# Fetching split keys and queries as float32 on both sides, rows outermost, on GpSimd's queue

## Chip, cores and metric

The kernel runs on one core of a Trainium2 chip. The metric is the device time of one execution in microseconds (us), the median of several runs; lower is better. TensorE (PE) does matrix products, VectorE (DVE) and ScalarE (ACT) the arithmetic on tiles, GpSimd (POOL) some of it too. SP, ACT and POOL each have a queue that issues DMA transfers, and 16 DMA engines carry them out.

## Reference

Two transformer blocks, batch 1, 1024 tokens, width 1024, float32. The first has two kinds of attention side by side (a latent one over all keys, "MLA", and a dilated window one), then a mixture of 16 experts. The second block is run twice ("layers"); each layer has three kinds of attention over 1024 tokens and 256 context tokens: a differential one, one with grouped queries, one with a neighbourhood window on a grid. Cut to the three that matter here:

```python
def diff_attend(q, k, v, lam):
    s = jnp.einsum('bqhmd,bkhmd->bhmqk', q, k).astype(jnp.float32) * (q.shape[-1] ** -0.5)
    p = jax.nn.softmax(s, axis=-1)
    a = (p[:, :, 0] - lam * p[:, :, 1]).astype(v.dtype)
    return jnp.einsum('bhqk,bkhd->bqhd', a, v)

def gqa_attend(q, k, v):
    ...
    s = jnp.einsum('bqhgd,bkhd->bhgqk', qg, k).astype(jnp.float32) * (d ** -0.5)
    p = jax.nn.softmax(s, axis=-1).astype(v.dtype)
    o = jnp.einsum('bhgqk,bkhd->bqhgd', p, v)
```

The softmax is sharp on these inputs, so scores are computed to nearly full float32: every query and key is split into a high part and a low part (float32r, the form that TensorE takes at full rate), and a score is a sum of products of the parts.

## The kernel before

**Split and stack.** The projections write the parts to DRAM. `stack_out` (L654) transposes a tile of queries or keys, rounds it to float32r (`H`), takes the rest (`L`), and SP stores both in DRAM arrays `st[key]`, declared float32, shaped [2 parts, blocks, 128 rows, tokens]. The keys are "Dq", "Dk" (dilated), "Mq", "Mk", "Mr" (MLA), "Aq", "Ak" (differential), "Bq", "Bk" (grouped), "Cq", "Ck" (neighbourhood). A block holds two heads of 64 rows. A row of part a is 1024 or 1280 float32 in a piece, 4 or 5 KB.

**Fetch.** The attention stages read them back into SBUF tiles, from GpSimd's queue, since the source is float32 and the tile float32r, so that each of these transfers is a cast. Three helpers do it. `ld_key` (L1874) fills a tile [128, 2, tokens] whose rows 0 to 63 and 64 to 127 both hold one head's key: for each part one transfer whose outermost dimension is a repeat of 2 (stride 0), then 64 rows. `ld_pair` (L1869) fills a query tile for two heads, whose upper half of rows is part 0 and whose lower half is part 1: one transfer for each head, outermost dimension the 2 parts. `ld_maps` (L1884) fills a 96-row tile for the differential stream in four transfers, two of them with the outermost dimension 2. Where the lower products are not wanted (`row`, the grouped stream's keys), the second part goes to rows 0 to 63 alone and a GpSimd operation fills four rows with ones. The MLA stream (`mla_pair`, L949) and the tile `Qm` of the grouped stream (L2162) have their own transfers, which already have rows outermost (`"a r c -> r a c"`).

**Planner.** The three attention stages (first block; second block, layers 0 and 1) are not written out by hand. `Plan` (L89) is given operations, each with a priority, the engines that may run it with a planned time on each, its predecessors, its buffers and, for a transfer, a planned DMA time. `run` (L155) simulates this with the planned numbers and emits the instructions in the order in which they start in its plan. On the chip each engine then runs its own list strictly in that order: an instruction whose data are late holds up all behind it. The planned time for a `ld_key` or `ld_pair` is 2.1 us on POOL and 1.5 to 3.6 us of DMA, plus 2 us, for `ld_maps` 4.2 us on POOL. The buffers are few: two key tiles (`xk`) and two query tiles (`xq`), two of `dk`, two of `ek`, one `eq`. A new key is fetched when the last product with an old one is done.

**Streams.** In the first block "m" (MLA, scores at L980) and "e" (dilated, scores at L1150) are interleaved, beside SP loads of the 1 MB weights `aw` for two matrix-vector products. In the second block "x" (first neighbourhood, scores L2269, products with values L2226; then grouped, scores L2186, L2190, L2191) and "d" (differential, scores L2027) are interleaved. Sums of exponentials (L1057) and differences (L1963 to L1966) go to POOL or DVE as the planner finds one free.

Of the kernel before, what the change touches and what calls it, by code (L numbers as in the profile page):

```python
# [19 lines left out]
P = 128  # L20
# [205 lines left out]
class Kern:  # L226
# [722 lines left out]
    def mla_pair(self, p):  # L949
# [10 lines left out]
        def key(i):  # L960
            K = buf("mk", X, [100, 2, S], F32R)

            def ld(e):
                nc.gpsimd.dma_start(K.t[:64], self.st["Mk"][:, p, 64 * i:64 * i + 64, :].rearrange("a r c -> r a c"))
                nc.gpsimd.dma_start(K.t[64:100], self.st["Mr"][:, 0].rearrange("a r c -> r a c"))
            return K, pl.op(p0 - self.q["lead"], {"pool": 2.1}, ld, [], [K], 2.2)
        Ks = [key(i) for i in range(2)]

        def part(g):
            p0 = self.at[X]  # L970
            Y = buf("my", X, [P, 4, P])
            fins = []
            for i in range(2):
                K, lk = Ks[i]
                Q = buf("mq", X, [100, 2, 512], F32R)
                lq = pl.op(p0 - self.q["lead"] + 15 * i, {"pool": 1.05}, lambda e, Q=Q, i=i: nc.gpsimd.dma_start(
                    Q.t[:96], self.st["Mq"][:, 2 * p + i, :, g * 512:(g + 1) * 512].rearrange("a r c -> r a c")), [], [Q], 1.1)

                def s1(j, c0, w, dst, Q=Q, K=K):
                    nc.tensor.matmul(dst, Q.t[:96, 0, j * P:(j + 1) * P], K.t[:96, 0, c0:c0 + w], start=True, stop=True)  # L980

                def st(kb, dst, Q=Q, K=K):
                    c = slice(kb * P, (kb + 1) * P)
                    nc.tensor.matmul(dst, K.t[:96, 0, c], Q.t[:96, 0, :], start=True, stop=False)
                    nc.tensor.matmul(dst, K.t[:96, 0, c], Q.t[:96, 1, :], start=False, stop=False)
                    nc.tensor.matmul(dst, K.t[:100, 1, c], Q.t[:100, 0, :], start=False, stop=True)
                cs = slice(i * 64, i * 64 + 64)
                fins.append(self.st_group(X, 3.05, NT, CH[:2], s1, st, 0.65, [Q, K], [lq, lk], Q, lambda Q=Q: Q.t[96:100, 0, :],
                                          V, lv, cs, Y, cs, "mPT", "mA", sm))
            pl.op(self.at[X], {"act": 0.1}, lambda e: self.put_y(Y.t, 4 * g, 4, p * P, P), fins, [Y], 1.5)  # L990
# [79 lines left out]
    def dilated(self, dp):  # L1070
# [13 lines left out]
        for i in range(2):  # L1084
# [14 lines left out]
            for h in range(4 * i, 4 * i + 4):  # L1099
                p0 = self.at[X]  # L1100
                if h % 2 == 0:
                    Q = buf("eq", X, [P, 2, S], F32R)
                    lq = pl.op(p0 - self.q["lead"], {"pool": 2.1}, lambda e, Q=Q, h=h: self.ld_pair(Q.t, "Dq", h // 2, 0, S), [], [Q], 2.9)
                    loads.append(lq)
                K = buf("ek", X, [P, 2, S], F32R)
                lk = pl.op(p0 - self.q["lead"], {"pool": 2.1}, lambda e, K=K, h=h: self.ld_key(K.t, "Dk", h // 2, h % 2, False), [], [K], 2.9)
                loads.append(lk)
# [760 lines left out]

    def ld_pair(self, Q, key, blk, c0, n):  # L1869

        for i in range(2):
            self.nc.gpsimd.dma_start(Q[:, i, :], self.st[key][:, blk, 64 * i:64 * i + 64, c0:c0 + n])

    def ld_key(self, HL, key, blk, i, row):  # L1874

        for a in range(2):
            src = self.st[key][a, blk, 64 * i:64 * i + 64, :]
            if a and row:
                self.nc.gpsimd.dma_start(HL[:64, a, :], src)
                self.pcopy(HL[64:68, a, :], self.ones[64:68].to_broadcast([4, S + 256]))  # L1880
                break
            self.nc.gpsimd.dma_start(HL[:, a, :], bass.AP(tensor=src.tensor, offset=src.offset, ap=[[0, 2]] + [list(x) for x in src.ap]))

    def ld_maps(self, A, key, h, c0, n):  # L1884


        r0 = (h % 2) * 64
        for i in range(2):
            src = self.st[key][:, h // 2, r0 + 32 * i:r0 + 32 * i + 32, c0:c0 + n]
            if key == "Aq":  # L1890
                self.nc.gpsimd.dma_start(A[:64, i, :], src)
                self.nc.gpsimd.dma_start(A[64:96, i, :], src[0])
            else:
                s0 = src[0]
                self.nc.gpsimd.dma_start(A[:64, i, :], bass.AP(tensor=s0.tensor, offset=s0.offset, ap=[[0, 2]] + [list(x) for x in s0.ap]))
                self.nc.gpsimd.dma_start(A[64:96, i, :], src[1])

# [46 lines left out]
    def stream_d(self, l, with_ctx):  # L1944
# [25 lines left out]
        def head(h):  # L1970
# [3 lines left out]
            Y, G_ = buf("dy", X, [P, 10, 64]), buf("dg", X, [P, 10, 64])  # L1974
            lk = pl.op(p0 - self.q["lead"], {"pool": 4.2}, lambda e: self.ld_maps(K.t, "Ak", h, 0, S + 256), [], [K], 2.7)
            lv = pl.op(p0 - self.q["lead"], {"sp": 0.1}, lambda e: self.part_cols(V.t, "A", 0, 10, h * 64, 64), [], [V], 0.9)
            fins = []

            def group(g):
                p0 = self.at[X]  # L1980
                Q = buf("dq", X, [96, 2, 512], F32R)
                lq = pl.op(p0 - self.q["lead"], {"pool": 4.2}, lambda e: self.ld_maps(Q.t, "Aq", h, g * 512, 512), [], [Q], 1.1)
                PT = buf("dPT", X, [P, 10, 4, P])
# [21 lines left out]
                if g == 0 and with_ctx:  # L2005
                    Qx = buf("dx", X, [96, 2, 256], F32R)
                    lx = pl.op(p0 - self.q["lead"], {"pool": 4.2}, lambda e: self.ld_maps(Qx.t, "Aq", h, 2 * 512, 256), [], [Qx], 0.6)
                    for gq in range(2):
                        fins.append(self.d_ctx(self.step(X, 1.0), gq, Qx, K, V, Y, [lx, lk, lv], coeff, combine, sm))
# [106 lines left out]
    def stream_x(self, l, with_ctx):  # L2116
# [6 lines left out]
        def pair(kind, p):  # L2123
# [10 lines left out]
            for i, k in enumerate(ks):  # L2134
                if (kind, k) not in keys:
                    K = buf("xk", X, [P, 2, S + 256], F32R)
                    keys[kind, k] = K, pl.op(at - self.q["lead"] + 8 * i, {"pool": 2.1}, lambda e, K=K, k=k: self.ld_key(
                        K.t, part + "k", k // 2, k % 2, kind == "B"), [], [K], 3.6)
                    loads.append(keys[kind, k][1])
# [9 lines left out]
            def part_(g):  # L2149
# [3 lines left out]
                    ("x", "xq", [2, n * P], F32R), ("xg", "xg", [n, P], F32), ("xy", "xy", [n, P], F32)))  # L2153
                lq = pl.op(at - self.q["lead"], {"pool": 2.1}, lambda e: self.ld_pair(Q.t, part + "q", p, g * 512, n * P), [], [Q], 1.5)
                loads.append(lq)
# [5 lines left out]
                else:  # L2161
                    Qm = buf("tb", X, [68, 2, 512], F32R)  # L2162
                    lm = pl.op(at - self.q["lead"], {"pool": 1.05}, lambda e: nc.gpsimd.dma_start(
                        Qm.t[:64], self.st["Bq"][0, p, :, g * 512:(g + 1) * 512].rearrange("(i r) c -> r i c", i=2)), [], [Qm], 0.7)
                    fins = [self.gqa_group(i, Q, Qm, K[i], V, vcol[i], Y, G_, [lq, lv, lg, lm], sm) for i in range(2)]
# [331 lines left out]
```

## Time and profile before

| | us |
|---|---|
| median of 3 runs | 3687.04 (3684.84 to 3689.37) |
| profiled execution, its own time | 3682.54 |
| its span in the trace | 3680.6 |
| PE busy | 3361.7 (91% of the span) |
| DVE busy | 2352.2 (64%) |
| ACT busy | 1710.7 (46%) |
| POOL busy | 1205.9 (33%) |

The attention stages lie at about 345 to 865 us, 2015 to 2565 us and 3080 to 3580 us of the span. In the rows, a bracket behind an instruction is how long its engine stood idle before it and what it waited for by the semaphores ("issue": nothing that the trace shows). "To landing" is the time from the issue of a transfer to its completion. PEclk is the TensorE clock that was granted, 1.00 for 2.4 GHz and 0.50 for 1.2 GHz.

### The profile page before, as it was taken

What the parts mean: (1) busy time and instruction counts of PE and PEld (TensorE: products, weight loads), DVE (VectorE), ACT (ScalarE), POOL (GpSimd) and SP (SyncE); (2) the same over time, 40 slices, a digit from 0 to 9 for tenths busy, and PEclk for the clock granted to TensorE, in tenths of its full rate; (3) what the DMA queues carried; (4) which work ended last, traced back from release to release, by engine and by line L of the source; (5) the groups of instructions that cost most, each with busy time, mean ns of one, the idle gap of its engine ahead of it and who ended that gap; (6) DMA issues with size and microseconds to landing.
All of it is one profiled execution on the core that took longest, in us unless ns stands there. A gap on an engine that the chain in (4) does not pass through costs nothing.

```text
span 3680.6 us, 51685 instructions
## 1 busy us (share of the span) xinstructions
PE 3361.7 (91%) x17880; PEld 2581.4 (70%) x17880; DVE 2352.2 (64%) x5558; ACT 1710.7 (46%) x3153; POOL 1205.9 (33%) x1069
## 2 busy tenths in 40 slices
PE   7998887889499999989999789999999999799999
PEld 5987555547388887779889555556899887465557
DVE  5525544444699998876841678887446814689962
ACT  4324444432288877653322566654333214565640
POOL 3111323232001001033530344565333512446661
PEclk9999898989699999989999899999999999899999
DMA  7348767666599999654452764213334445542133
GB/s 201 97 118 230 178 153 176 149 199 216 208 381 396 396 393 373 234 168 124 132 149 62 134 110 84 50 38 123 120 125 127 120 136 111 114 94 51 42 106 109
DMA packets 533178, 600.72 MB, mean 163 GB/s; under 512 B 203218, under 2 KB 409426, under 8 KB 528818
## 3 DMA queue, kind: packets, MB, share of 16 engines
q1 hardware_dynamic: 339828, 486.92, 40.2%
q0 software_dynamic: 160768, 94.63, 13.2%
q10 hardware_dynamic: 32320, 15.86, 1.6%
q8 instruction: 142, 2.33, 0.3%
q14 instruction: 120, 0.98, 0.1%
HBM read 473.33 MB, written 123.50 MB: 162 GB/s over the span
## 4 chain that ended last, share of the span: by engine, by line
PE 55%; DVE 7%; DMA 7%; POOL 2%; issue 2%; ACT 2%; SPq 0%; ACTq 0%; DVEq 0%; POOLq 0%
PE s L349 6%; PE s L350 6%; PE s L348 6%; PE a L350 6%; PE a L349 6%; PE a L348 6%; PE t L316 5%; PE o L1931 4%; DMA xk<-stackCk 3%; PE o L2226 2%; PE s L2027 2%; PE s L2186 1%; PE s L2269 1%; DMA xk<-stackBk 1%; PE t L1939 1%
## 5 line engine op out<-in xcount | busy, mean ns | idle before, releaser
L348 PE MATMUL a<-wh,h2H 128*128 128x384 f32 (+2 forms) x1328 | 477.1, 359 | 8.2 <-ACT vd L1608 5.0
L350 PE MATMUL a<-wh,h2L 128*128 128x384 f32 (+2 forms) x1328 | 470.3, 354 | 3.6 <-POOL h2L L596 3.6
L349 PE MATMUL a<-wl,h2H 128*128 128x384 f32 (+2 forms) x1328 | 469.9, 354 | 1.3 <-DVE wl L335 1.3
L1481 DVE TENSOR_TENSOR wl<-wr,wh 128x1024 fp32r<-128x1024 f32 x384 | 450.4, 1221 | 25.9 <-ACT wh L1480 19.2
L1480 ACT ACTIVATE wh<-wr 128x1024 fp32r<-128x1024 f32 x384 | 395.9, 1059 | 77.3 <-PE s L350 74.7
L348 PEld LDWEIGHTS a<-wh,h2H 128*128 128x128 f32 x1328 | 252.5, 190 | 30.0 <-ACT vd L1608 5.4
L350 PEld LDWEIGHTS a<-wh,h2L 128*128 128x128 f32 x1328 | 252.2, 190 | 27.1 <-POOL h2L L596 5.0
L349 PEld LDWEIGHTS a<-wl,h2H 128*128 128x128 f32 x1328 | 252.6, 190 | 22.7 <-DVE wl L335 1.6
L1861 DVE CUSTOM_DVE_ANT_0 dP<-s,zero 128x512 f32<-128x512 f32 (+1 forms) x384 | 218.0, 595 | 23.2 <-PE s L2027 22.1
L349 PE MATMUL s<-wl,xH 128*128 128x512 f32 x512 | 201.5, 394 | 4.5 <-DVE wl L1481 4.2
L348 PE MATMUL s<-wh,xH 128*128 128x512 f32 x512 | 202.2, 395 | 0.0
L350 PE MATMUL s<-wh,xL 128*128 128x512 f32 x512 | 199.8, 390 | 0.0
L2049 ACT ACTIVATE dP<-dP,d 128x1280 f32<-128x1280 f32 x128 | 174.2, 1363 | 44.2 <-DVE d L2043 41.0
L1057 POOL TENSOR_TENSOR xP<-xP,xPT 128x512 f32<-128x512 f32 x130 | 181.8, 1398 | 36.1 <-DVE xP L1057 12.5
L1020 DVE TENSOR_REDUCE x<-s 128x1 f32<-128x512 f32 (+1 forms) x240 | 157.2, 683 | 22.2 <-PE s L2186 21.6
L348 PE MATMUL s<-wh,yoH 128*128 128x512 f32 x416 | 166.6, 402 | 1.5 <-DVE yo L2406 0.8
L349 PE MATMUL s<-wl,yoH 128*128 128x512 f32 x416 | 165.8, 399 | 0.8 <-DVE wl L335 0.8
L350 PE MATMUL s<-wh,yoL 128*128 128x512 f32 x416 | 164.6, 396 | 0.0
L1053 ACT ACTIVATE xPT<-t 128x512 f32<-128x512 f32 x240 | 130.0, 604 | 72.9 <-PE t L2191 63.5
L335 POOL TENSOR_TENSOR wl<-wr,wh 128x1024 fp32r<-128x1024 f32 (+3 forms) x43 | 93.9, 2183 | 209.9 <-ACT wh L333 205.7
L2269 PE MATMUL s<-xk,xq 128*128 128x512 f32 (+2 forms) x480 | 106.9, 341 | 47.8 <-issue 30.9
L1463 POOL DMA_INDIRECT xg<-h2d,idx x16 | 16.4, 1027 | 400.8 <-PE t L316 326.5
(456 smaller groups left out, 8355.6 us busy)
## 6 DMA issues: line engine op xcount, KB each, us to landing
wr<-in_w_gate_dram SPq DMA_DIRECT2D x128, 512.0 KB
wr<-in_w_up_dram SPq DMA_DIRECT2D x128, 512.0 KB
wr<-in_w_down_dram SPq DMA_DIRECT2D x128, 512.0 KB
aw<-in_w_ada_dram SPq DMA_DIRECT2D x32, 1024.0 KB
wr<-in_w_in_dram SPq DMA_DIRECT2D x44, 512.0 KB
aw<-in_w_ada_dram SPq DMA_DIRECT2D x32, 512.0 KB
xk<-stackCk POOLq DMA_DIRECT2D x24, 640.0 KB, 23.6
wr<-in_w_in_dram SPq DMA_DIRECT2D x36, 384.0 KB
```

The costliest lines, as they stand in the source:

```text
L316: self.nc.tensor.transpose(out, in_, self.ident[:n, :n])
L348: nc.tensor.matmul(out, sH, h, start=first, stop=False)
L349: nc.tensor.matmul(out, sH, l, start=False, stop=False)
L350: nc.tensor.matmul(out, sL, h, start=False, stop=last)
L1020: nc.vector.tensor_reduce(dst, Sb.t[:, :n * w].rearrange("p (k c) -> p k c", k=n) if n > 1 else Sb.t[:, :w], AX.X, ALU.max)
L1057: eng.tensor_tensor(A.t[:, :512], PT.t[:, 0, :] if kb == 1 else A.t[:, :512], PT.t[:, kb, :], ALU.add)
L1480: nc.scalar.activation(h, raw, AF.Copy)
L1481: nc.vector.tensor_tensor(l, raw, h.bitcast(F32), ALU.subtract)
L1861: self.nc.vector.tensor_tensor_reduce(dst, src, self.zero.to_broadcast(list(src.shape)), 1.0, -3e38, ALU.add, ALU.max, m)
L1931: nc.tensor.matmul(O.t[a * 64:(a + 1) * 64, :], v(kb), PT[0](kb), start=(kb < 2), stop=(kb >= nb - 2))
L2049: nc.scalar.activation(Ps[i].t, Ps[i].t, AF.Exp, bias=b["m"][:, i:i + 1], accum_out=box[j][:, i:i + 1])
L2269: nc.tensor.matmul(Sb[a].t[:, c:c + n], q, K.t[:, h, lo * P + k0:lo * P + k0 + n], start=(h == 0), stop=(h == 1))
```

## The change

All fetches of split keys and queries go through a helper that views the destination tile as float32, so that source and destination have one type; they stay on GpSimd's queue (`e` is "pool" for each of these operations). The transfers are cut anew, so that the outermost dimension of each is rows: `ld_key` makes two transfers of 64 rows with both parts in each (where `row` is set, the second has part 0 alone), `ld_pair` makes one for each part of 64 rows with both heads, `ld_maps` makes three of 32 rows with both maps in place of four. What lies in SBUF afterwards is the same. The planned POOL times go from 2.1 to 1.4, from 1.05 to 0.7 and from 4.2 to 2.0 us; the planned DMA times stay.

```diff
@@ mla_pair
             def ld(e):
-                nc.gpsimd.dma_start(K.t[:64], self.st["Mk"][:, p, 64 * i:64 * i + 64, :].rearrange("a r c -> r a c"))
-                nc.gpsimd.dma_start(K.t[64:100], self.st["Mr"][:, 0].rearrange("a r c -> r a c"))
-            return K, pl.op(p0 - self.q["lead"], {"pool": 2.1}, ld, [], [K], 2.2)
+                self.fetch(e, K.t[:64], self.st["Mk"][:, p, 64 * i:64 * i + 64, :].rearrange("a r c -> r a c"))
+                self.fetch(e, K.t[64:100], self.st["Mr"][:, 0].rearrange("a r c -> r a c"))
+            return K, pl.op(p0 - self.q["lead"], {"pool": 1.4}, ld, [], [K], 2.2)
...
-                lq = pl.op(p0 - self.q["lead"] + 15 * i, {"pool": 1.05}, lambda e, Q=Q, i=i: nc.gpsimd.dma_start(
-                    Q.t[:96], self.st["Mq"][:, 2 * p + i, :, g * 512:(g + 1) * 512].rearrange("a r c -> r a c")), [], [Q], 1.1)
+                lq = pl.op(p0 - self.q["lead"] + 15 * i, {"pool": 0.7}, lambda e, Q=Q, i=i: self.fetch(
+                    e, Q.t[:96], self.st["Mq"][:, 2 * p + i, :, g * 512:(g + 1) * 512].rearrange("a r c -> r a c")), [], [Q], 1.1)
@@ helpers
-    def ld_pair(self, Q, key, blk, c0, n):
-
-        for i in range(2):
-            self.nc.gpsimd.dma_start(Q[:, i, :], self.st[key][:, blk, 64 * i:64 * i + 64, c0:c0 + n])
-
-    def ld_key(self, HL, key, blk, i, row):
+    def fetch(self, e, dst, src):
+
+        (self.nc.sync if e == "sp" else self.nc.gpsimd).dma_start(dst.bitcast(F32), src)
+
+    def ld_pair(self, e, Q, key, blk, c0, n):
 
         for a in range(2):
-            src = self.st[key][a, blk, 64 * i:64 * i + 64, :]
-            if a and row:
-                self.nc.gpsimd.dma_start(HL[:64, a, :], src)
-                self.pcopy(HL[64:68, a, :], self.ones[64:68].to_broadcast([4, S + 256]))
-                break
-            self.nc.gpsimd.dma_start(HL[:, a, :], bass.AP(tensor=src.tensor, offset=src.offset, ap=[[0, 2]] + [list(x) for x in src.ap]))
-
-    def ld_maps(self, A, key, h, c0, n):
+            self.fetch(e, Q[64 * a:64 * a + 64], self.st[key][a, blk, :, c0:c0 + n].rearrange("(i r) c -> r i c", i=2))
+
+    def ld_key(self, e, HL, key, blk, i, row):
+
+        src = self.st[key][:, blk, 64 * i:64 * i + 64, :].rearrange("a r c -> r a c")
+        self.fetch(e, HL[:64], src)
+        self.fetch(e, HL[64:, :1] if row else HL[64:], src[:, :1] if row else src)
+        if row:
+            self.pcopy(HL[64:68, 1, :], self.ones[64:68].to_broadcast([4, S + 256]))
+
+    def ld_maps(self, e, A, key, h, c0, n):
 
 
         r0 = (h % 2) * 64
-        for i in range(2):
-            src = self.st[key][:, h // 2, r0 + 32 * i:r0 + 32 * i + 32, c0:c0 + n]
-            if key == "Aq":
-                self.nc.gpsimd.dma_start(A[:64, i, :], src)
-                self.nc.gpsimd.dma_start(A[64:96, i, :], src[0])
-            else:
-                s0 = src[0]
-                self.nc.gpsimd.dma_start(A[:64, i, :], bass.AP(tensor=s0.tensor, offset=s0.offset, ap=[[0, 2]] + [list(x) for x in s0.ap]))
-                self.nc.gpsimd.dma_start(A[64:96, i, :], src[1])
+        for b, a in enumerate((0, 1, 0) if key == "Aq" else (0, 0, 1)):
+            self.fetch(e, A[32 * b:32 * b + 32], self.st[key][a, h // 2, r0:r0 + 64, c0:c0 + n].rearrange("(i r) c -> r i c", i=2))
```

The calls in `dilated`, `stream_d` and `stream_x` change in the same way (2.1 to 1.4 for `ld_key` and `ld_pair`, 4.2 to 2.0 for `ld_maps`, 1.05 to 0.7 for `Qm`).

## Rows read from the trace of the kernel before

**Rows 1.** Waits of PE, whole span: who for whom, total us, times, longest
```profile
PE s L2269 <- issue: 30.9, 4, 11.5
PE s L1150 <- issue: 20.9, 2, 10.6
...
PE s L980 <- DMA mq<-stackMq: 16.5, 4, 10.0
PE s L2269 <- DMA xk<-stackCk: 15.9, 5, 11.3
...
PE o L2226 <- DMA xv<-partC: 10.1, 1, 10.1
...
PE t L316 <- ACT oT L1855: 6.9, 2, 5.6
```

**Rows 2.** Timeline of PE, five places: start, us, instruction, idle before it
```profile
603.57 2.47 PE L980 MATMUL s<-mk,mq 96*128 96x512 f32 x5 [9.99 <-DMA mq<-stackMq]
...
651.13 2.23 PE L1150 MATMUL s<-ek,eq 128*128 128x256 f32 x8 [10.61 <-issue]
...
2085.02 0.77 PE L2269 MATMUL s<-xk,xq 128*128 128x512 f32 x1 [11.53 <-issue]
...
2193.09 0.76 PE L2269 MATMUL s<-xk,xq 128*128 128x512 f32 x1 [11.33 <-DMA xk<-stackCk]
...
2288.71 0.69 PE L316 MATMUL t<-ident,dP 128*128 128x128 f32 x2 [5.55 <-ACT oT L1855]
```

**Rows 3.** DMA issues, whole span: count, KB of each, median us to landing
```profile
xk<-stackCk POOLq DMA_DIRECT2D x24, 640.0 KB, 23.6
...
ek<-stackDk POOLq DMA_DIRECT2D x16, 512.0 KB, 21.1
...
mk<-stackMk POOLq DMA_DIRECT2D x8, 512.0 KB, 7.2
```

**Rows 4.** Timeline of POOL, at five places of the attention stages
```profile
457.28 0.64 POOL L964 DMA_DIRECT2D mk<-stackMk  x1 [0.99 <-PE t L986]
...
459.80 0.67 POOL L976 DMA_DIRECT2D mq<-stackMq  x1
...
631.40 1.63 POOL L1872 DMA_DIRECT2D eq<-stackDq  x2 [11.27 <-PE t L316]
...
2061.01 1.63 POOL L1882 DMA_DIRECT2D xk<-stackCk  x2 [0.28 <-issue]
...
2165.64 1.59 POOL L1882 DMA_DIRECT2D xk<-stackCk  x2 [0.24 <-PE s L2269]
```

**Rows 5.** `mk`, `mr` then `mq`, 455 to 462 us: us to landing
```profile
DMA to landing us min/median/max: 7.2/7.3/7.5
...
DMA to landing us min/median/max: 6.9/6.9/6.9
```

**Rows 6.** Windows: us, busy of PE, PEld, DVE, ACT, POOL, clock, DMA share, GB/s
```profile
529.20:537.20 8.00, 7.96 (x34) 5.65 (x35) 1.38 (x2) 1.52 (x3) 0.00 (x0) 0.61 0.59 174
...
3291.90:3299.90 8.00, 7.98 (x40) 5.37 (x40) 5.69 (x14) 3.02 (x7) 3.03 (x3) 0.79 0.77 122
...
2104.00:2160.00 56.00, 55.74 (x366) 37.60 (x366) 49.01 (x189) 40.26 (x84) 27.16 (x32) 1.00 0.41 87
350.00:860.00 510.00, 428.96 (x2448) 281.10 (x2447) 243.22 (x607) 209.46 (x542) 153.38 (x138) 0.90 0.69 179
2015.00:2560.00 545.00, 490.03 (x2691) 308.87 (x2689) 439.28 (x1279) 321.51 (x654) 285.06 (x284) 0.93 0.43 87
3080.00:3575.00 495.00, 452.02 (x2481) 280.77 (x2479) 398.99 (x1195) 290.48 (x539) 280.76 (x260) 0.96 0.41 87
```

**Rows 7.** Timeline of POOL, 2270 to 2285 us: a wait for a landing
```profile
2283.00 0.66 POOL L1895 DMA_DIRECT2D dk<-stackAk  x1 [10.16 <-DMA xk<-stackBk]
```

**Rows 8.** Groups of POOL's DMA issues: busy us, mean ns of one, idle before
```profile
L1882 POOL DMA_DIRECT2D xk<-stackCk x24 | 19.6, 834 | 17.8 <-PE s L2269 17.0 <-POOL qd L1694 0.6 <-issue 0.3
...
L964 POOL DMA_DIRECT2D mk<-stackMk x8 | 5.1, 640 | 13.4 <-DVE eB L1156 10.9 <-PE t L986 1.7 <-PE t L316 0.7
```

More of the change, by code (lines that the diff above doesn't have):

```diff
@@ L1102, in dilated @@
                     Q = buf("eq", X, [P, 2, S], F32R)
-                    lq = pl.op(p0 - self.q["lead"], {"pool": 2.1}, lambda e, Q=Q, h=h: self.ld_pair(Q.t, "Dq", h // 2, 0, S), [], [Q], 2.9)
+                    lq = pl.op(p0 - self.q["lead"], {"pool": 1.4}, lambda e, Q=Q, h=h: self.ld_pair(e, Q.t, "Dq", h // 2, 0, S), [], [Q], 2.9)
                     loads.append(lq)
                 K = buf("ek", X, [P, 2, S], F32R)
-                lk = pl.op(p0 - self.q["lead"], {"pool": 2.1}, lambda e, K=K, h=h: self.ld_key(K.t, "Dk", h // 2, h % 2, False), [], [K], 2.9)
+                lk = pl.op(p0 - self.q["lead"], {"pool": 1.4}, lambda e, K=K, h=h: self.ld_key(e, K.t, "Dk", h // 2, h % 2, False), [], [K], 2.9)
                 loads.append(lk)
@@ L1974, in head @@
             Y, G_ = buf("dy", X, [P, 10, 64]), buf("dg", X, [P, 10, 64])
-            lk = pl.op(p0 - self.q["lead"], {"pool": 4.2}, lambda e: self.ld_maps(K.t, "Ak", h, 0, S + 256), [], [K], 2.7)
+            lk = pl.op(p0 - self.q["lead"], {"pool": 2.0}, lambda e: self.ld_maps(e, K.t, "Ak", h, 0, S + 256), [], [K], 2.7)
             lv = pl.op(p0 - self.q["lead"], {"sp": 0.1}, lambda e: self.part_cols(V.t, "A", 0, 10, h * 64, 64), [], [V], 0.9)
@@ L1981, in group @@
                 Q = buf("dq", X, [96, 2, 512], F32R)
-                lq = pl.op(p0 - self.q["lead"], {"pool": 4.2}, lambda e: self.ld_maps(Q.t, "Aq", h, g * 512, 512), [], [Q], 1.1)
+                lq = pl.op(p0 - self.q["lead"], {"pool": 2.0}, lambda e: self.ld_maps(e, Q.t, "Aq", h, g * 512, 512), [], [Q], 1.1)
                 PT = buf("dPT", X, [P, 10, 4, P])
@@ L2006, in group @@
                     Qx = buf("dx", X, [96, 2, 256], F32R)
-                    lx = pl.op(p0 - self.q["lead"], {"pool": 4.2}, lambda e: self.ld_maps(Qx.t, "Aq", h, 2 * 512, 256), [], [Qx], 0.6)
+                    lx = pl.op(p0 - self.q["lead"], {"pool": 2.0}, lambda e: self.ld_maps(e, Qx.t, "Aq", h, 2 * 512, 256), [], [Qx], 0.6)
                     for gq in range(2):
@@ L2136, in pair @@
                     K = buf("xk", X, [P, 2, S + 256], F32R)
-                    keys[kind, k] = K, pl.op(at - self.q["lead"] + 8 * i, {"pool": 2.1}, lambda e, K=K, k=k: self.ld_key(
-                        K.t, part + "k", k // 2, k % 2, kind == "B"), [], [K], 3.6)
+                    keys[kind, k] = K, pl.op(at - self.q["lead"] + 8 * i, {"pool": 1.4}, lambda e, K=K, k=k: self.ld_key(
+                        e, K.t, part + "k", k // 2, k % 2, kind == "B"), [], [K], 3.6)
                     loads.append(keys[kind, k][1])
@@ L2153, in part_ @@
                     ("x", "xq", [2, n * P], F32R), ("xg", "xg", [n, P], F32), ("xy", "xy", [n, P], F32)))
-                lq = pl.op(at - self.q["lead"], {"pool": 2.1}, lambda e: self.ld_pair(Q.t, part + "q", p, g * 512, n * P), [], [Q], 1.5)
+                lq = pl.op(at - self.q["lead"], {"pool": 1.4}, lambda e: self.ld_pair(e, Q.t, part + "q", p, g * 512, n * P), [], [Q], 1.5)
                 loads.append(lq)
@@ L2162, in part_ @@
                     Qm = buf("tb", X, [68, 2, 512], F32R)
-                    lm = pl.op(at - self.q["lead"], {"pool": 1.05}, lambda e: nc.gpsimd.dma_start(
-                        Qm.t[:64], self.st["Bq"][0, p, :, g * 512:(g + 1) * 512].rearrange("(i r) c -> r i c", i=2)), [], [Qm], 0.7)
+                    lm = pl.op(at - self.q["lead"], {"pool": 0.7}, lambda e: self.fetch(
+                        e, Qm.t[:64], self.st["Bq"][0, p, :, g * 512:(g + 1) * 512].rearrange("(i r) c -> r i c", i=2)), [], [Qm], 0.7)
                     fins = [self.gqa_group(i, Q, Qm, K[i], V, vcol[i], Y, G_, [lq, lv, lg, lm], sm) for i in range(2)]
```

## The prediction

> **What bounds the kernel now.** I read the page's busy shares first (they stand in the table above): PE is busy for 91% of the span, no other engine for more than 64%. So only what frees PE can shorten the program, and the question is what PE's idle time in the three attention stages waits for, as the change touches nothing outside them. The view of who waits for whom answers that [rows 1]. The score products of the neighbourhood stream (L2269) stood idle for 30.9 us behind "issue" and 15.9 us behind landings of `xk`; those of the dilated stream (L1150) for 20.9 us behind "issue"; the MLA scores (L980) for 16.5 us behind landings of `mq`. "issue" says only that the trace shows no releaser. The timeline shows that it is a fetch [rows 2, 4]: two transfers of an `xk` key are issued from 2061.01 us on, PE comes to the first product with that key at 2073.49 us (2085.02 less 11.53), 12.5 us after the issue, and stands.
>
> Why the fetches are late is in the view of DMA issues [rows 3]: the median `xk` transfer of 640 KB takes 23.6 us to land and an `ek` of 512 KB 21.1 us, but `mk`, of the same 512 KB and the same queue, 7.2 us. All are casts. What differs is the outermost dimension: a repeat of 2 in `xk` and `ek`, 64 rows in `mk`. The trace doesn't show which DMA engines a transfer runs on, but a factor of three at equal size is what a transfer held to few of them would give. The change gives every fetch the shape of `mk`.
>
> Last the windows [rows 6]. Between stalls PE is the bound: 55.74 of 56 us busy from 2104 to 2160 us at clock 1.00, with DVE at 49.01. So a stall there is lost time, and removed it is mostly gained. After a stall comes a second loss: in the 8 us behind each the granted clock averages 0.61 (first) to 0.79 (last), below the 1.00 of undisturbed stretches, that is, a part of each runs at the 1.2 GHz level.
>
> **The change part by part.**
>
> *Landing of a key or query.* Removed: outermost dimensions of 2. How long does a new pair of key transfers (1.28 MB) take? Nearest rows: `mk` (512 KB) is issued at 457.28 us, `mr` (288 KB) right behind, `mq` (384 KB) at 459.80; the first two land at most 7.5 us after their issue and `mq` 6.9 us after its own, at 466.7 [rows 4, 5]. So 1.18 MB came in 9.4 us, SP's weight loads beside them. Scaled by bytes, 1.28 MB takes about 10 us; from below, 7.2 us [rows 3], from above the 23.6 us of today. I take 10, as the rows it comes from have the same shape and queue. PE comes to the two `xk` stalls of rows 2 at 12.5 us and (2193.09 less 11.33, less 2165.64) 16.1 us after the issue: both vanish.
>
> *The stalls one by one.* L2269 gives 30.9 + 15.9 = 46.8 us. L1150 gives 20.9 us, but not all: `eq` and `ek` are fetched together, 2 MB, from 631.40 us on, and PE arrives at 640.52, 9.1 us later; at the rate above 2 MB need 16 us, at twice that rate 8. I leave 5 us of the two L1150 stalls standing, so 15.9 us are gained. Of L980's 16.5 us the 9.99 us at 603.57 count; the rest of this row are `mq` transfers whose shape the change doesn't touch. That one had the same shape too, but stood behind an `ek` of 1 MB of the old shape and beside 1 MB weight loads; I count it in full. Sum 72.7 us.
>
> *Two indirect stalls.* PE stood 10.1 us for `xv` [rows 1], an SP transfer that shares the DMA engines with `dk` and `dq` fetches of the old shape at the start of a layer; spread over all engines these leave none of them clogged. And 5.55 us at 2288.71 [rows 2]: POOL's next DMA issue stood 10.16 us until an `xk` landed [rows 7] (it looks as if only so many transfers may be in flight on its queue), and the sums behind it on POOL, for which PE waited, came late. Faster landing frees POOL's queue. Together 15.7 us, sum 88.4.
>
> *The clock.* Ten windows of 8 us, one behind each long stall (the first and last stand in rows 6), have a mean clock of 0.70, so (1 - 0.70) x 80 = 24 us of work were lost. Sum 112 us.
>
> *What takes the place.* After a stall the other engines had caught up; without it, PE meets them sooner. In layer 0 DVE is busy 439.28 of 545 us and PE 490.03 [rows 6]; 545 - 60 = 485 us would put DVE at 91%, above the 87.5% (49.01 of 56) of the undisturbed stretch. So small waits for DVE will open. I take off a quarter, for this and for waits that a static order meets elsewhere: **83 us**. The ends: nothing taken off, and the 5 us of L1150 too, 117 us; two thirds taken off, 37 us.
>
> *POOL's issue time.* An `xk` issue takes 834 ns, an `mk` issue 640 [rows 8]; some 130 transfers get 0.2 us cheaper and 28 `ld_maps` lose one of four. POOL is busy a third of the span, so I cost it at nothing; what covers it is the idle time of POOL. Nothing in the rows suggests that an issue gets dearer.
>
> *No cast.* The trace of before has no direct transfer without a cast on this queue. From below, it costs what `mk` does with it; a gain is not excluded, nor a loss. I take zero; a landing some microseconds off changes only the L1150 stalls, by 5 us either way.
>
> *The planner.* Some 120 operations get 0.35 to 2.2 us shorter in the plan, so the emitted order of all three stages changes somewhat, and POOL may get a few more of the sums from DVE. I cost this at zero, +-15 us.
>
> *A rule that speaks against it.* In the rows, `mk` and `mr` go to different rows of one tile, 64 and 36 of them, follow one another by 0.63 us and land within 0.3 us of the same delay, 7.2 and 7.5 us [rows 5]: they overlap. The Trainium skill (DMA: Bandwidth & Descriptors, section Rules for kernel authors) holds that two transfers to disjoint partition halves serialize and advises one transfer over 128 partitions, which is what `ld_key` and `ld_pair` had and give up. By that rule the gain would be that of rival 2.
>
> **How the numbers stand to the runs.** The sum is made on the profiled execution, 3682.54 us; the median of the runs is 4.5 us above it. 3687 - 83 = 3604.
>
> **Rivals.**
> 1. *Everything goes.* No quarter is lost, and POOL's freed queue and the planner's new order bring more: 112 to 140 us, 3547 to 3575. For it: PE is the bound between stalls [rows 6]. Against: DVE at 91%. Chance 0.12.
> 2. *The halves queue up behind each other.* A half key of 640 KB takes 7.2 x 640/512 = 9 us and the second lands 18 us after the issue. The two `xk` stalls at 12.5 and 16.1 us keep 5.5 and 1.9 us, all of L2269 some 12 us; `eq` with `ek`, four halves of 7.2 us, needs 29 us where PE arrives after 9.1, about 9 us worse than now at each of two places. Saved: 46.8 - 12 + 10 + 15.7 - 18 = 42.5 us, with half of the clock 54.5, less a quarter 41: 3646. Against it stand rows 5, where such halves overlapped. This is what the rule above would give. Chance 0.07.
> 3. *The stalls turn mostly into others.* PE meets DVE, at 87.5% already between stalls [rows 6], or a worse order, and two thirds of the 112 us come back: 37 us gained, 3650, between 3630 and 3677. For it: the stages' order is static. Chance 0.17.
> 4. *Slower: fetches hold up SP's loads.* A fetch now occupies all engines, so a load on SP's queue for which PE waits comes late by up to the time of the fetch, 7 to 10 us, instead of being slowed on few engines. It decides if it hits PE's weight loads `aw` or `tb`, `xv` more often than stalls vanish: at ten places, 10 us each with the clock behind, 100 us less 83: 3704. Against: DMA share is 0.43 and 0.41 in layers 0 and 1 [rows 6], so such loads have room. Chance 0.05.
> 5. *The shape isn't what slows the fetch*, or the direct transfer is spread no better: 3687 +-7, from the new order alone. Against: `mk`. Chance 0.05.
>
> **Chances and range.** The forecast, 3572 to 3630, has 0.54, the rivals 0.12, 0.07, 0.17, 0.05 and 0.05. No change within 0.2% (7.4 us, about what a measurement of this kernel can tell from none) takes most of rival 5 and nothing else: 0.04. Slower: rival 4 and the rest of rival 5, 0.06. Faster 0.90. The range leaves out about half of rival 1, some of rivals 2 and 3, and all of 4 and 5, some 0.2 together: 3553 to 3664.
>
> **What would show it.** Landing of `xk` and `ek` at 7 to 12 us; `mk` and `mq` hardly changed. PE's waits at L2269 for "issue" and `xk` under 8 us in all, at L1150 under 8, the 10 us before L2226 for `xv` and POOL's 10 us wait for `xk` gone. PEclk of layer 0 from 0.93 to 0.97 or more, its stage some 45 us shorter, layer 1 about 20, the first block's stage about 20. Outside the attention stages nothing moves. Wrong would be the forecast if landings stay over 15 us (rival 2 or 5), if they fall and PE stands as long before DVE's results, or if waits for SP's loads grow (rival 4).

## The result, and the profile after

The changed kernel takes 3581.62 us (median of 4 runs, 3575.55 to 3593.31) against 3687.24 us before on the same chip: ratio 0.9718 [0.9692, 0.9743], so about 105 us faster, where 83 us were forecast. The profiled execution took 3575.55 us.

First the page's busy shares, its clock line and the row of POOL's DMA queue (packets, MB, share of the span of 16 engines).

```profile
span 3573.6 us, 51656 instructions
...
PE 3341.9 (94%) x17880; PEld 2572.3 (72%) x17880; DVE 2359.4 (66%) x5555; ACT 1703.9 (48%) x3138; POOL 1221.0 (34%) x1071
...
PEclk9999999999699999999999999999999999999999
...
q0 software_dynamic: 26240, 94.13, 11.3%
```

The page before has PE at 3361.7 us of a span of 3680.6. The same 17880 matmuls took 19.8 us less, which I put down to the clock. The rest is idle time, 318.9 us before and 231.7 after, 87.2 less. Together 107.0, the difference of the two spans. So the two numbers say where the time came from before any wait is read.

Next the DMA issues (count, KB each, median us to landing), which answer to [rows 3].

```profile
xk<-stackCk POOLq DMA_DIRECT2D x24, 640.0 KB, 8.5
ek<-stackDk POOLq DMA_DIRECT2D x16, 512.0 KB, 10.8
dk<-stackAk POOLq DMA_DIRECT2D x24, 320.0 KB, 5.9
mq<-stackMq POOLq DMA_DIRECT2D x16, 384.0 KB, 5.8
...
mk<-stackMk POOLq DMA_DIRECT2D x8, 512.0 KB, 6.0
```

`xk` lands in 8.5 us instead of 23.6, `ek` in 10.8 instead of 21.1; `mk`, whose shape the change leaves as it was, moved from 7.2 to 6.0. Then the waits of PE (total us, times, longest), which answer to [rows 1].

```profile
PE s L980 <- DMA mq<-stackMq: 14.8, 6, 7.0
...
PE o L2221 <- DMA xv<-partC: 8.9, 1, 8.9
...
PE s L467 <- DMA aw<-in_w_ada_dram: 6.2, 2, 4.5
```

The score products of the neighbourhood stream (now L2264) and of the dilated one (L1150) no longer wait for a fetch anywhere. What stayed is `xv` (L2221, before L2226) and part of `mq`. The windows of the three attention stages (columns as in [rows 6]) show the clock and PE's share. They run from the first score product of a stage to the first transpose of its result behind it, so that each holds the same products before (first three lines) and after:

```profile
340.24:817.88 477.64, 400.52 (x2323) 261.49 (x2321) 231.84 (x610) 200.71 (x536) 147.93 (x137) 0.89 0.69 172
2015.31:2564.00 548.69, 493.19 (x2705) 312.03 (x2705) 439.76 (x1279) 321.51 (x654) 285.06 (x284) 0.93 0.44 89
3083.17:3577.24 494.07, 451.72 (x2476) 280.79 (x2477) 398.80 (x1194) 289.99 (x538) 280.44 (x260) 0.96 0.41 88
```

```profile
337.02:771.02 434.00, 393.45 (x2323) 260.12 (x2321) 230.15 (x608) 197.00 (x521) 153.53 (x145) 0.94 0.68 190
1962.24:2480.92 518.68, 487.61 (x2705) 309.29 (x2705) 435.19 (x1273) 318.46 (x645) 302.14 (x291) 0.96 0.37 93
2999.64:3469.75 470.11, 448.52 (x2476) 278.76 (x2477) 407.99 (x1199) 290.40 (x547) 277.67 (x248) 0.97 0.36 92
```

The clock rose from 0.89, 0.93 and 0.96 to 0.94, 0.96 and 0.97. The first block's stage got 43.6 us shorter, layer 0 30.0, layer 1 24.0, and the rest of the program 9.4.

### The profile page after: what moved, and what is told of

Same layout as the page of the kernel before. It is cut to its first block, busy times and chain, and to the rows that moved or that the text cites. A ratio compares the mean times of both kernels' runs of the same rounds, so it can differ in the third digit from the quotient of the medians.

```text
span 3573.6 us, 51656 instructions
## 1 busy us (share of the span) xinstructions
PE 3341.9 (94%) x17880; PEld 2572.3 (72%) x17880; DVE 2359.4 (66%) x5555; ACT 1703.9 (48%) x3138; POOL 1221.0 (34%) x1071
## 3 DMA queue, kind: packets, MB, share of 16 engines
q0 software_dynamic: 26240, 94.13, 11.3%
## 5 line engine op out<-in xcount | busy, mean ns | idle before, releaser
L350 PEld LDWEIGHTS a<-wh,h2L 128*128 128x128 f32 x1328 | 250.9, 189 | 28.5 <-POOL h2L L596 6.4
L2044 ACT ACTIVATE dP<-dP,d 128x1280 f32<-128x1280 f32 x128 | 174.1, 1363 | 52.8 <-DVE d L2038 43.6
L1057 POOL TENSOR_TENSOR xP<-xP,xPT 128x512 f32<-128x512 f32 x118 | 164.3, 1393 | 38.8 <-DVE xP L1057 21.7
L335 DVE TENSOR_TENSOR wl<-wr,wh 128x1024 fp32r<-128x1024 f32 (+3 forms) x55 | 73.7, 1342 | 114.4 <-ACT wh L333 114.4
```

The lines of the kernel that those rows point to most:

```text
L335: e.tensor_tensor(l, raw, h.bitcast(F32), ALU.subtract)
L350: nc.tensor.matmul(out, sL, h, start=False, stop=last)
L1057: eng.tensor_tensor(A.t[:, :512], PT.t[:, 0, :] if kb == 1 else A.t[:, :512], PT.t[:, kb, :], ALU.add)
L2044: nc.scalar.activation(Ps[i].t, Ps[i].t, AF.Exp, bias=b["m"][:, i:i + 1], accum_out=box[j][:, i:i + 1])
```

## The experiments

My theory was that the outermost dimension sets the landing and that the landing makes the gain. Its rivals: the cast that is left out, the new POOL times in the plan and with them another order, the number of transfers, the queue. Each was changed alone. The ratio is to the kernel before, run on the same chip beside it. The sessions were on different chips, where the kernel before had medians from 3680 to 3694 us, so a difference between two sessions is good to some 10 us.

| kernel | median us | ratio, 95% |
|---|---|---|
| changed kernel | 3581.62 | 0.9718 [0.9692, 0.9743] |
| cast_rows | 3584.52 | 0.9711 [0.9675, 0.9746] |
| nocast_two | 3738.57 | 1.0126 [1.0080, 1.0171] |
| plan_only | 3732.29 | 1.0104 [1.0064, 1.0145] |
| rows_oldplan | 3563.80 | 0.9662 [0.9627, 0.9698] |
| mixed | 3559.22 | 0.9647 [0.9631, 0.9663] |
| rows_longplan | 3589.53 | 0.9733 [0.9712, 0.9754] |
| halves64 | 3608.53 | 0.9802 [0.9785, 0.9820] |
| outer8, one run | 3659.73 | |
| outer4, one run | 3693.45 | |
| maps_two | 3631.14 | 0.9856 [0.9838, 0.9874] |
| sp_same | 3593.22 | 0.9760 [0.9743, 0.9777] |
| sp_first | 3565.26 | 0.9687 [0.9666, 0.9707] |

**cast_rows**: the changed kernel with the cast back in.

```diff
     def fetch(self, e, dst, src):
-        (self.nc.sync if e == "sp" else self.nc.gpsimd).dma_start(dst.bitcast(F32), src)
+        (self.nc.sync if e == "sp" else self.nc.gpsimd).dma_start(dst, src)
```

> The change with the cast put back (tile as float32r), rows outermost, new plan times, so the same order of instructions as the changed kernel. Theory (the outermost dimension decides): xk lands in 8 to 11 us, time 3575 to 3600 us. Rival (the cast is what was slow): xk lands in over 15 us, time over 3640 us.

Measured 3584.52 us, 2.9 above the changed kernel with overlapping runs. `xk` lands in 9.0 us, `ek` in 11.3. The queue's row has more packets and a little more engine time than the changed kernel's:

```profile
q0 software_dynamic: 34880, 94.13, 12.8%
```

Leaving out the cast is worth nothing that can be measured here.

**nocast_two**: no cast and the new plan, but the transfers cut as before.

```diff
     def ld_key(self, e, HL, key, blk, i, row):
-        src = self.st[key][:, blk, 64 * i:64 * i + 64, :].rearrange("a r c -> r a c")
-        self.fetch(e, HL[:64], src)
...
+        for a in range(2):
+            src = self.st[key][a, blk, 64 * i:64 * i + 64, :]
...
+            self.fetch(e, HL[:, a, :], bass.AP(tensor=src.tensor, offset=src.offset, ap=[[0, 2]] + [list(x) for x in src.ap]))
```

(`ld_pair` and `ld_maps` likewise.)

> The transfers cut as before (outermost dimension 2), but without the cast, in the order of the changed kernel. Theory (outermost dimension): xk lands in over 20 us, time 3670 to 3710 us, and PE stands some 60 us or more for fetches again. Rival (the cast): landing under 12 us, time under 3610 us.

Measured 3738.57 us: slower than the kernel before and above the range. The landings are back where they were (columns as above), and PE's waits show the fetches, and beside them a wait that the kernel before has for 1.2 us only:

```profile
xk<-stackCk POOLq DMA_DIRECT2D x24, 640.0 KB, 23.5
ek<-stackDk POOLq DMA_DIRECT2D x16, 512.0 KB, 20.9
```

```profile
PE t L316 <- POOL dP L1969: 37.1, 7, 13.8
...
PE s L2272 <- DMA xk<-stackCk: 19.4, 7, 9.3
...
PE s L2272 <- issue: 14.1, 1, 14.1
```

So the cut does the work: with the new plan it is worth 154 us (3738.57 less 3584.52, where both differ in the cast too, which cost nothing). The `dP` wait is the next question: the new plan is in this kernel.

**plan_only**: the kernel before with nothing but the new POOL times in the plan.

```diff
-            return K, pl.op(p0 - self.q["lead"], {"pool": 2.1}, ld, [], [K], 2.2)
+            return K, pl.op(p0 - self.q["lead"], {"pool": 1.4}, ld, [], [K], 2.2)
...
-            lk = pl.op(p0 - self.q["lead"], {"pool": 4.2}, lambda e: self.ld_maps(K.t, "Ak", h, 0, S + 256), [], [K], 2.7)
+            lk = pl.op(p0 - self.q["lead"], {"pool": 2.0}, lambda e: self.ld_maps(K.t, "Ak", h, 0, S + 256), [], [K], 2.7)
```

(and so on at all ten places of the change.)

> The kernel before with the new planned POOL times alone. Theory: 3670 to 3700 us, xk still lands in over 20 us. Rival (the new order brings the gain): under 3640 us.

**rows_oldplan** is its mirror: the changed kernel with the old times at those ten places (`{"pool": 1.4}` back to `2.1`, `2.0` to `4.2`, `0.7` to `1.05`).

> The change with the old planned POOL times (2.1, 1.05, 4.2 us), so the order of instructions of the kernel before. Theory: landings as after, time 3575 to 3605 us; the plan is worth under 15 us either way. Rival (the new order brings the gain): over 3640 us.

Measured: plan_only 3732.29 us, 38 above the kernel before (3694.34 in that session), rows_oldplan 3563.80 us, 21 below cast_rows of the same session. Both lie outside the ranges given for them, plan_only above, rows_oldplan below: the plan was to be worth under 15 us. So the new plan costs time under both cuts, more under the old one. (Plan_only and cast_rows have the cast and the new plan in common and differ in the cut alone: 148 us.) PE's waits of plan_only, and the groups of POOL instructions (busy us, mean ns of one | idle before) in it and in "mixed", a kernel below with the old plan in the layers, show what it does:

```profile
PE t L316 <- POOL dP L1966: 33.9, 8, 13.0
PE s L980 <- DMA mq<-stackMq: 31.6, 7, 10.6
```

```profile
L1966 POOL TENSOR_TENSOR dP<-dP,dP 128x1280 f32<-128x1280 f32 x43 | 127.8, 2971 | 3.6
```

```profile
L1961 POOL TENSOR_TENSOR dP<-dP,dP 128x1280 f32<-128x1280 f32 x26 | 76.2, 2932 | 2.2
```

A planner that thinks an issue cheap gives POOL 43 differences of the `d` stream instead of 26. On POOL each takes 2.97 us, and POOL does them in order between its DMA issues. Where its queue stands for slow landings, they come late and PE waits (33.9 us here, 37.1 in nocast_two). The longest of these waits in nocast_two, on POOL and then on PE:

```profile
2171.79 0.67 POOL L1871 DMA_DIRECT2D dk<-stackAk  x1 [9.05 <-DMA xk<-stackCk]
...
2178.77 2.88 POOL L1969 TENSOR_TENSOR dP<-dP,dP 128x1280 f32<-128x1280 f32 x1
...
2181.70 2.39 PE L316 MATMUL t<-ident,dP 128*128 128x128 f32 x10 [13.83 <-POOL dP L1969]
```

Where landings are fast, this wait is gone (0.6 us in the changed kernel), but the order still costs some 20 us. They lie in the layers: by the landmarks above, the two layers take 518.7 and 470.1 us in the changed kernel, 506.4 and 458.8 in rows_oldplan. No single wait holds them. PE's waits for DVE in the two layers add up to 29.0 us instead of 18.0, and PE is busy about 10 us longer for the same products; which operations of the new order bring this isn't shown.

**mixed** takes the new times in the first block only and the old ones in the two layers.

```diff
@@ stream_d, stream_x
-            lk = pl.op(p0 - self.q["lead"], {"pool": 2.0}, lambda e: self.ld_maps(e, K.t, "Ak", h, 0, S + 256), [], [K], 2.7)
+            lk = pl.op(p0 - self.q["lead"], {"pool": 4.2}, lambda e: self.ld_maps(e, K.t, "Ak", h, 0, S + 256), [], [K], 2.7)
...
-                    keys[kind, k] = K, pl.op(at - self.q["lead"] + 8 * i, {"pool": 1.4}, lambda e, K=K, k=k: self.ld_key(
+                    keys[kind, k] = K, pl.op(at - self.q["lead"] + 8 * i, {"pool": 2.1}, lambda e, K=K, k=k: self.ld_key(
```

> The change, with its new planned POOL times in the first block's stage and the old ones in the two layers. Theory (the new plan hands 17 more differences dP of the differential stream to GpSimd, and that is what it costs): the loss is in the layers alone, time 3545 to 3570 us, at or under the 3564 of the change with the old plan throughout. Rival (the orders differ by chance in all three stages): 3565 to 3590 us.

Measured 3559.22 us (3552.26 to 3564.07), ratio 0.9647 [0.9631, 0.9663]: the best of all, below both kernels, its interval apart from the changed kernel's. Against rows_oldplan it is no more than equal (3560.91 to 3568.82). The layers take 506.8 and 458.9 us, as in rows_oldplan, so the loss is in the layers, as the theory had it; that it is the differences on POOL isn't shown by this, since the whole order of the layers changes with them.

**rows_longplan** goes the other way: planned POOL times longer than the old ones (3.0, 1.5 and 6.0 us), to see whether a planner that thinks POOL dear does better still.

```diff
-            lk = pl.op(p0 - self.q["lead"], {"pool": 2.0}, lambda e: self.ld_maps(e, K.t, "Ak", h, 0, S + 256), [], [K], 2.7)
+            lk = pl.op(p0 - self.q["lead"], {"pool": 6.0}, lambda e: self.ld_maps(e, K.t, "Ak", h, 0, S + 256), [], [K], 2.7)
```

> The change with planned POOL times longer than either (3.0, 1.5 and 6.0 us). Theory (the planner is to be pessimistic about POOL, since its queue also stands for landings and a difference there is slow): dP on POOL 20 or fewer, time 3545 to 3565 us. Rival (a truthful plan is best and the old numbers were lucky): over 3575 us.

Measured 3589.53 us, with 23 differences on POOL. It is no faster than the changed kernel, and the theory's range (3545 to 3565 us, 20 or fewer) is missed on both counts. So fewer differences on POOL isn't by itself what gains, and the time as a function of the planned cost isn't monotone. Nor does the rival hold that a truthful plan is best, since mixed is faster than the changed kernel. Why the old values do best isn't shown.

**outer4, outer8, halves64**: is it the outermost dimension, and by degrees? Each sends one part of one half per transfer, twice as many transfers as the changed kernel; outer4 and outer8 order the rows so that the outermost dimension is 4 or 8 (the same on both sides of every product), halves64 leaves it at 64 (32 for the maps).

```diff
+    def spread(self, e, dst, src):
+        for k in range(src.shape[1]):
+            self.fetch(e, dst[:, k, :], src[:, k, :].rearrange("(r o) c -> o r c", o=4))
...
-        self.fetch(e, HL[:64], src)
+        self.spread(e, HL[:64], src)
```

(outer8 has `o=8`; halves64 has `self.fetch(e, dst[:, k, :], src[:, k, :])`.)

> The changed kernel with every fetch of the dilated, differential, neighbourhood and grouped streams cut to one part of one half per transfer, and its rows taken in the order that makes the outermost dimension 4 (queries and keys alike, so the scores are the same sums). Theory (a transfer runs on as many DMA engines as its outermost dimension allows, up to 16): a key's bytes move half as slowly as with 2 and 4 times as slowly as with 16; xk lands in 12 to 18 us, time between 3600 and 3690 us. Rival (only a repeat or a split of parts outermost is slow, not the number): xk lands as after the change, 8 to 10 us.

> As outer4 with the outermost dimension 8. Theory: xk lands in 9 to 13 us, between outer4 and the change. Rival: 8 to 10 us and no different from outer4.

> Twice as many transfers as in the changed kernel, each of one part of one half (320 KB for an xk), outermost dimension still rows (64 or 32). The control for outer4 and outer8, which issued the same number. Theory (the outermost dimension sets the landing, the number of transfers costs only POOL's issue time): xk lands in 6 to 9 us, POOL's issues grow by some 130 x 0.6 = 80 us in all but are hidden, the program takes 3570 to 3610 us, well below outer4's 3693 and outer8's 3660. Rival (outer4 and outer8 lost their time by issuing twice as often, which holds up POOL's sums): 3640 to 3700 us, with PE waiting for POOL's differences dP for 15 us or more.

The `xk` rows of the DMA issues and PE's wait for POOL's differences, in outer4, outer8 and halves64 in turn:

```profile
xk<-stackCk POOLq DMA_DIRECT2D x48, 320.0 KB, 13.8
```

```profile
xk<-stackCk POOLq DMA_DIRECT2D x48, 320.0 KB, 9.2
```

```profile
xk<-stackCk POOLq DMA_DIRECT2D x48, 320.0 KB, 7.1
```

```profile
PE t L316 <- POOL dP L1965: 39.2, 8, 14.0
```

```profile
PE t L316 <- POOL dP L1965: 17.4, 8, 7.3
```

```profile
PE t L316 <- POOL dP L1965: 11.3, 8, 3.0
```

At equal size and equal number of transfers the landing falls from 13.8 over 9.2 to 7.1 us as the outermost dimension goes from 4 over 8 to 64, and the time from 3693 over 3660 to 3609. The Trainium skill (DMA: Bandwidth & Descriptors, section Rules for kernel authors) holds that an outermost dimension under 16 confines a transfer to at most as many DMA engines; the runs agree in the order, though 4 against 8 gave a factor of 1.5 and not of 2. So the theory holds for the landings; of the times, halves64 lies at the top of its range and outer4 3 us above it. The rival has a part in it, though: halves64 stands 27 us above the changed kernel, with POOL busy for 1309.2 us instead of 1221.0, 11.3 us of waits of PE for its differences, and 18.1 us instead of 4.4 for ACT's `xP`, for which ACT in turn waits 18.8 us for POOL. The rest of outer4's loss, 85 us, and of outer8's, 51 us, is the dimension's, by one run of each.

How many engines the fetches keep busy can be read where nothing else is under way. The row of POOL's queue before, from 2286.0 to 2288.5 us, with only the `dk` transfers issued from 2283.00 us on [rows 7], and after, from 2017.0 to 2024.3 us, with two of `xk` and two of `xq`:

```profile
q0 software_dynamic: 17, 0.09, 15.2%
```

```profile
q0 software_dynamic: 371, 1.59, 98.3%
```

15.2% of 16 engines are 2.4 engines; after, nearly all are busy. That is the tail of one transfer, though. Before, from 2064 to 2073 us, with up to six transfers of the old shape under way (`xk` and `xq`), q0 keeps 72.6% of the engines busy and moves only 0.93 MB, and 3256 of the stretch's 3501 packets are under 512 bytes. So the old shape leaves engines idle at one place and has busy ones move little at another, and these runs don't part the two.

**maps_two**: the changed kernel, with the coefficient maps `dk`, `dq`, `dx` alone cut as before.

```diff
     def ld_maps(self, e, A, key, h, c0, n):
         r0 = (h % 2) * 64
-        for b, a in enumerate((0, 1, 0) if key == "Aq" else (0, 0, 1)):
-            self.fetch(e, A[32 * b:32 * b + 32], self.st[key][a, h // 2, r0:r0 + 64, c0:c0 + n].rearrange("(i r) c -> r i c", i=2))
+        for i in range(2):
+            src = self.st[key][:, h // 2, r0 + 32 * i:r0 + 32 * i + 32, c0:c0 + n]
+            if key == "Aq":
+                self.fetch(e, A[:64, i, :], src)
+                self.fetch(e, A[64:96, i, :], src[0])
...
```

> The changed kernel with the coefficient maps dk, dq and dx alone fetched as before (four transfers, outermost dimension 2 for two of them), without a cast; keys and queries stay in rows. Theory (each stream's fetches cost where PE meets them, and the time of before went mainly to xk, ek and what queued behind them on POOL): dk lands slower, 10 us or more, PE waits for a dk or dq or for POOL's dP by 15 to 50 us more, the total is 3590 to 3640 us. Rival (the maps lie far enough ahead): within 10 us of the changed kernel, 3570 to 3592 us.

Measured 3631.14 us, 50 above the changed kernel. But PE doesn't wait for a map at all, and for `dP` 1.7 us. It stands for others' transfers. The timelines of PE and of POOL around the longest stall, then the landings:

```profile
1998.04 1.98 PE L2228 MATMUL o<-xPT,xv 128*64 128x256 f32 x8 [11.25 <-DMA xv<-partC]
...
3169.41 1.62 PE L2271 MATMUL s<-xk,xq 128*128 128x512 f32 x4 [18.49 <-issue]
```

```profile
3132.57 2.40 POOL L1871 DMA_DIRECT2D dk<-stackAk  x4
...
3152.50 1.23 POOL L1871 DMA_DIRECT2D xk<-stackCk  x2
```

```profile
xk<-stackCk POOLq DMA_DIRECT2D x24, 640.0 KB, 12.5
...
dk<-stackAk POOLq DMA_DIRECT2D x16, 320.0 KB, 16.9
```

`xk` has the new cut here, and still its median landing rose from 8.5 to 12.5 us; the stall of 18.49 us ends 16.9 us after an `xk` issue. The total came as the theory had it, the place did not: a badly shaped transfer costs the well-shaped ones beside and behind it. The maps themselves show it too: the second `dk` transfer of the old cut has 160 KB with 32 rows outermost, and it lands in 16.7 us here and in 13.9 before, as late as the first, of 320 KB with the outermost dimension 2 (16.9 and 14.0).

**sp_same**: the changed kernel with all fetches issued on SP's queue, in the same order of the plan.

```diff
-        (self.nc.sync if e == "sp" else self.nc.gpsimd).dma_start(dst.bitcast(F32), src)
+        self.nc.sync.dma_start(dst.bitcast(F32), src)
```

> The changed kernel with every fetch issued on SP's queue in place of GpSimd's, same plan, same order. Theory (it is the outermost dimension that counts, the queue doesn't): xk lands in 7 to 11 us, the total is 3560 to 3610 us, and POOL's waits for landings and its issues (some 0.6 us each) are gone. Rival A (SP issues in order, so a fetch that waits for its buffer holds up the weight loads and xv behind it): PE's waits for aw, tb or xv grow beyond 40 us, the total is over 3620 us. Rival B (POOL's queue and its issue time still cost what is left): 20 to 40 us faster than the changed kernel, 3540 to 3560 us.

Measured 3593.22 us, 12 above the changed kernel and 90 below the one before: the queue doesn't matter much, and rivals A and B fall. (The profile gives no landing for these issues.) One row wasn't forecast: there is no wait for `xv` at all, but 10.2 us for `dq` (4.1 of them in layer 0). There the first `xv` is issued at 1968.47 us, `dk` behind it at 1973.42, and the first product with `xv` runs at 1977.9, at most 9.4 us after the issue. In the changed kernel `xv` is issued at 1963.85, beside `dk`, `dq` and `dx` from 1962.52 on, and PE gets it 18.9 us later:

```profile
1982.76 0.69 PE L2221 MATMUL o<-xPT,xv 128*64 128x256 f32 x2 [8.88 <-DMA xv<-partC]
```

**sp_first** tests that alone: "mixed" with the first head's maps of each layer on SP's queue, where they stand behind `xv`.

```diff
-            self.fetch(e, A[32 * b:32 * b + 32], self.st[key][a, h // 2, r0:r0 + 64, c0:c0 + n].rearrange("(i r) c -> r i c", i=2))
+            self.fetch("sp" if h == 0 else e, A[32 * b:32 * b + 32], self.st[key][a, h // 2, r0:r0 + 64, c0:c0 + n].rearrange("(i r) c -> r i c", i=2))
```

> The kernel 'mixed' with the maps of each layer's first head (dk, dq, dx: 12 transfers in layer 0, 9 in layer 1) issued on SP's queue, which puts them behind the loads xv and xg in layer 0; everything else, the order on PE, DVE and ACT too, as in 'mixed'. Theory (xv lands late at the start of layer 0 because dk, dq and dx in flight share the DMA engines with its 512-byte packets): xv lands in at most 12 us instead of 18.9, PE's wait for it falls from 8.8 to under 3 us, the total is 3548 to 3559 us. Rival A (xv is late by itself, 1280 small packets behind the copies into partC): the wait stays at 7 to 10 us, the total within 5 us of mixed's 3559.2. Rival B (the maps are now late): the xv wait goes, waits for dk or dq of 5 to 12 us take its place, the total is 3555 to 3567 us.

The timeline of SP in sp_first, and the waits of PE in it:

```profile
1976.04 0.74 SPq L1864 DMA_DIRECT2D xv<-partC  x1
...
1980.90 3.41 SPq L1871 DMA_DIRECT2D dk<-stackAk  x3
```

```profile
PE s L2022 <- DMA dq<-stackAq: 11.5, 2, 6.2
```

The wait for `xv` is gone (the first product with it runs at 1986.0 us, 10 us after the issue, not 18.9), so the theory of its lateness holds. But PE now waits 6.2 us for `dq` at 1996.35 instead of 8.8 us for `xv`, and 5.3 us for it in layer 1, and the total is 3565.26 us, no better than mixed: rival B. In those 20 us everything that the layer needs is under way at once, and here the order only picks who is late.

## Why the prediction was right, and where it was not

**The landing step held.** A pair of `xk` halves was to land in about 10 us; at 2015.40 us the changed kernel issues two, and the view of `xk` in that stretch gives

```profile
DMA to landing us min/median/max: 5.9/7.1/8.3
```

that is, both within 8.9 us of the first issue. The second half doesn't wait for the first, as rival 2 had it (18 us, and 3646 us in all). The Trainium skill (DMA: Bandwidth & Descriptors, section Rules for kernel authors) holds that two transfers to disjoint partition halves serialize and advises one transfer over 128 partitions; the two halves here don't follow one another, but no run has one transfer over 128 partitions with rows outermost to set against them. That the shape and not the cast makes the difference was taken from one comparison, `mk` against `xk`; nocast_two and cast_rows show it.

**The stalls.** L2269's 46.8 us went in full, as forecast. L1150's 20.9 us went in full, where 5 us were left standing. For `mq`, L980's landings and "issue" (16.5 and 7.7 us before) became 14.8 us, 9.4 less, where 9.99 us were counted. That the size came out is in part luck: the same waits are 16.3 us in mixed and 12.3 in sp_first, with the same order in the first block. POOL's 10.16 us of [rows 7] are gone: its issues stand 8.7 us in all for landings of earlier fetches, before 60.6. Not forecast: PE's waits for `aw` at L467 fell from 15.9 to 6.2 us. That is not the cut alone, since rows_oldplan has 15.4, and not settled as the plan's, since mixed, with the new plan there, has 10.4.

**The step on `xv` failed.** "Spread over all engines these leave none of them clogged": the wait for it went from 10.1 to 8.9 us only. DMA rows of 8 us in which `xv` is under way, before (2025 to 2033 us) and after (1976 to 1984); the first line is the busy share in 40 slices, then packets, MB, share of each queue:

```profile
DMA  9999999949856756668584966576767543423138
...
q0 software_dynamic: 1040, 0.75, 68.0%
q1 hardware_dynamic: 324, 0.13, 13.0%
```

```profile
DMA  9989899999999999989997999899999998989989
...
q0 software_dynamic: 388, 1.21, 66.7%
q1 hardware_dynamic: 1252, 0.62, 40.9%
```

Before, part of the engines' time was idle and `xv`'s queue (q1) still moved little; after, all engines are full, and q1's packets of some 500 bytes share them with the fetches on q0. This is the mechanism of rival 4, at one place and not at ten; PE waits for no other transfer in the two layers.

**The clock** was sized right: 24 us forecast, 19.8 by PE's busy time, 28.5 with the old plan (rows_oldplan, 3333.2 us).

**Two terms were off, in opposite directions.** The first is the quarter of 112 us (28; the sum takes 29) taken off for "small waits for DVE". By the cut alone it was not lost: PE's waits for DVE in the two layers add up to 17.5 us before and 18.0 in rows_oldplan. In the changed kernel they are 29.0, so 11.5 us of this term did come, but by the new plan and not by the stalls that went. DVE was to reach 91% of layer 0; it is busy for 435.19 of 518.68 us, 84%, and with the old plan in "mixed" for 418.61 of 490, 85%. The second is the planner. Costed at zero +-15, it costs 21 us with the new cut and 38 us with the old.

The cut at the old plan gains 130.5 us (3694.34 less 3563.80), which is near the top of rival 1's 112 to 140; in the profiled executions it is 121.9 (93.4 of idle time, 28.5 of busy PE), against the 112 of the sum ahead of the quarter and the 5 of L1150. The planned times gave some 20 us of it back. So the sum was nearly right for the cut, and the quarter ought not to have come off. That the time fell between 3572 and 3630 us is in part luck: without the planner's loss it would have lain below, where rival 1 was.

**By stage**, the first block gained 43.6 us where about 20 were forecast (20.9 of L1150, 9.4 of `mq`, 9.7 of `aw`, and the clock). Some of it belongs to the one execution that was profiled: mixed and sp_first have the same order there and take 443.9 and 439.2 us for this stage, not 434.0. Layer 0 gained 30.0 instead of 45 and layer 1 24.0 instead of 20; with the old plan (rows_oldplan) they gain 42.3 and 35.3. So layer 0 was sized right for the cut and layer 1 too low, and the new plan took some 12 us from each. The 9.4 us outside the stages, where nothing was to move, are no more than two runs of one kernel differ by.

## What to carry to other kernels

Compare the landing of transfers of equal size on one queue: a factor of three between them points at the access pattern, and the outermost dimension is the first thing to look at, ahead of casts and queues. A badly shaped transfer is paid by its neighbours too, so mend all of a stream's fetches, not only the one that PE waits for. When a planner or a cost table orders the work, a changed cost is a change of its own: time it apart from the change it comes with, also when the new cost is closer to the truth.

## What the runs showed of the hardware that I had not expected

The old cut makes many tiny packets. With the cast in both, queue q0 has 160768 packets and 94.63 MB before and 34880 packets and 94.13 MB in cast_rows: 125888 packets more for 0.50 MB, about 4 bytes each. Without the cast, nocast_two has 112768, outer4 72768, outer8 43968 and the changed kernel 26240. So they go with the outermost dimension, and the cast adds to them (48000 with the old cut, 8640 with the new). Whether they are a cause of the slow landing or only its companion isn't settled by these runs.

POOL's queue stands behind its own earlier landings: before, a `dk` issue stood 10.16 us until an `xk` had landed [rows 7], and in outer4 a `dq` issue stood 11.4 us for an `xk`. In all, its issues stand 60.6 us for landings of earlier fetches before, 81.1 in nocast_two, 80.9 in plan_only and 59.0 in outer4, against 8.7 in the changed kernel. Where landings are late this reaches the arithmetic on POOL, as the `dP` waits of nocast_two, plan_only and outer4 show; where landings are short it costs next to nothing.
